# Stores of ScalarE's PSUM copies issued by ScalarE's own queue instead of SyncE's, in a hybrid RWKV-7, SSD and GLA block

## Chip, cores and metric

The kernel runs on one core of a Trainium2 chip. The metric is the device time of one execution in microseconds (us); three executions before the change had a median of 1492.69 us, from 1491.11 to 1495.21 us.

## What is computed

One trunk layer of a diffusion backbone, all in float32. A latent stream of 1024 tokens with 1024 channels and a context of 256 tokens are normalized, projected by one matrix, and handed to three groups of heads; the concatenated results go through an output projection and a residual, and a mixture of 16 experts (two per token) and a final norm follow. The change touches the RWKV-7 group, cut down here to what matters:

```python
def step(s, inp):                       # rwkv7_scan, 4 heads of 64, run forwards and backwards
    r_t, w_t, k_t, v_t, a_t, b_t = inp
    sa = jnp.einsum('bhvk,bhk->bhv', s, a_t)
    s = s * w_t[:, :, None, :] + sa[..., None] * b_t[:, :, None, :] + v_t[..., None] * k_t[:, :, None, :]
    return s, jnp.einsum('bhvk,bhk->bhv', s, r_t)
...
decay = exp(-exp(-softplus(-(w0[d] + wl @ w2[d])) - 0.5)); a = sigmoid(a0[d] + al @ a2[d])
kk = k * k_k / norm; scan_inputs = (r, decay, k * (1 + (a - 1) * k_a), v, -kk, kk * a)
```

## The kernel before

The scan is computed in chunks of 64 tokens. `rw_seg` prepares a segment of 256 tokens (four chunks) for one pair of heads (b, 0 or 1) and both directions (d). There are five segments, so `rw_seg` goes 20 times through its inner loop; each such pass is called a segment pass here. In a segment pass TensorE transposes v into `ptv`, ScalarE copies it out of PSUM into `vt` (L433), and SyncE stores it to DRAM as `vtD` (L434). TensorE then makes `psl` in two halves (L438), ScalarE takes tanh into `sa` (L440), VectorE scans it into `cum` (L446), GpSimd subtracts (`cex`, L447), ScalarE takes three or four exps (L449 to L454), VectorE and GpSimd multiply them into `AR` and `BK`, and TensorE multiplies these into `psg` (L475), which VectorE masks into `G` (L477). GpSimd scales `BK` (L485), TensorE transposes it into `ptb` (L490), and ScalarE copies it into `BT` (L491), which has one buffer. SyncE stores `BT` to `stepD` by four DMAs of 64 KB (L496, here called a quartet). `AR` and `G` are stored by SyncE too (L481 to L483).

DRAM hands these results to later stages. `rw_inverse` reads `mabD` into `Dm`, inverts blocks on VectorE (lines L546 and L547 in turn, then the copy `DT`, L550), stores and reloads them as `t1` and `t2`, and multiplies them on TensorE as `px` (L575) and `px2` (L580). It runs three times; "inverse 2" is the one for positions 0 to 3 of both b, and the last but one in time. The scan loop `rw_step` reads `stepD` (L592) and `vtD` (L600); it begins when all jobs are through.

Around these, other jobs fill the engines: input projections (`psi`, L274 to L276, copied by ScalarE into `po` or `u`), convolutions (`co`, L751 on VectorE, after L740 on ScalarE), conditioning products (`psa`, L201, and `psc`, L206), and projections for GLA and SSD (`pst`, L274 to L276 as well). A job list fixes the order in which the program is written:

```python
PLAN = "s0 z0 z1 s1 z3 q0 z2 z5 z4 q1 c1 i0 g0 i2 c0 a4 a5 c3 a6 a7 c2 a8 a9 c5 a10 a11 t0 i1 c4"
...
with _tile.TileContext(nc, schedule_with_timeline_sim=True) as tc:
```

(s is a segment job with ten segment passes, i an inverse, c a convolution, a a conditioning product, t the GLA and SSD projection.) The order on each engine is not the written one. A scheduler takes the written program and decides when each instruction goes into its engine's line, so that a change of one queue can move instructions on all engines. Each engine runs its line strictly in order.

Of the kernel before, what the change touches and what calls it, by code (L numbers as in the profile page):

```python
# [48 lines left out]
def sigma(eng, out, t):  # L49

    eng.tensor_scalar(out, t, 0.5, 0.5, op0=OP.mult, op1=OP.add)
# [276 lines left out]
HS = [slice(0, 64), slice(64, 128)]  # L328


def chunks(t):
    return t.rearrange("p (c t) -> p c t", t=64)


def flip(v, d):
    return v[:, ::-1, ::-1] if d else v
# [76 lines left out]
def rw_seg(g, b, s, r, k, v, wa, kk):  # L413

    nc = g.nc
    t0, n, pos = SEGS[s]
    T = lambda tag, bufs=2, w=256: g.tmp.tile([128, w], F, tag=tag, name=tag, bufs=bufs)
    ts = slice(t0, t0 + n)
    r, k, v, wa, kk = r[:, ts], k[:, ts], v[:, ts], wa[:, ts], kk[:, ts]
    nch = n // 64  # L420
    for d in range(2):
        p0, bd = pos[d], 2 * b + d
        pp = slice(p0, p0 + nch)
        if d:
            vd = T("sq")[:, 0:n]
            nc.scalar.activation(vd[:, ::-1], v, AF.Copy)
        else:
            vd = v
        pt = g.ps.tile([128, 4, 128], F, tag="tp", name="ptv")
        for i in range(n // 128):  # L430
            nc.tensor.transpose(pt[:, i, :], vd[:, 128 * i:128 * i + 128], g.ident)
        vt = T("vt", 2, 258)[:, 0:n].rearrange("p (i c) -> p i c", c=128)
        nc.scalar.activation(vt, pt[:, 0:n // 128], AF.Copy)  # L433
        nc.sync.dma_start(g.vtD[pp, :, 128 * bd:128 * bd + 128].rearrange("(i q) t c -> (q t) i c", q=2), vt)  # L434
        ps = g.ps.tile([128, 2, 256], F, tag="tp", name="psl")
        sa = T("sa", 2, 512).rearrange("p (q t) -> p q t", q=2)
        for q in range(2):
            nc.tensor.matmul(ps[:, q, :], g.wa2[64 * q:64 * q + 64, d, 128 * b:128 * b + 128],  # L438
                             wa[64 * q:64 * q + 64], start=True, stop=True)
            nc.scalar.activation(sa[:, q, :], ps[:, q, :], AF.Tanh, scale=0.5,  # L440
                                 bias=g.hb[:, 4 * q + 2 * d + b:4 * q + 2 * d + b + 1])
        sigma(nc.vector, sa, sa)
        sig, av = sa[:, 0, :], sa[:, 1, :]
        cum, cex = T("cum")[:, 0:n], T("cex")[:, 0:n]
        rv = (lambda x: x[:, ::-1]) if d else (lambda x: x)
        nc.vector.tensor_tensor_scan(rv(cum), g.m01[:, 0:n], rv(sig), 0.0, op0=OP.mult, op1=OP.add)  # L446
        nc.gpsimd.tensor_sub(cex, cum, sig)  # L447

        nc.scalar.activation(cex, cex, AF.Exp, scale=-KAPPA)  # L449
        dst = g.PC[:, bd, p0:p0 + nch]  # L450
        nc.scalar.activation(dst[:, ::-1] if d else dst, chunks(cum)[:, :, 0 if d else 63], AF.Exp, scale=-KAPPA)
        if s:
            nc.scalar.activation(sig, cum, AF.Exp, scale=-KAPPA)
        nc.scalar.activation(cum, cum, AF.Exp, scale=KAPPA)  # L454
        ar = T("AR", 2, 512).rearrange("p (c a t) -> p c a t", a=2, t=64)[:, 0:nch]
        nc.vector.scalar_tensor_tensor(flip(ar[:, :, 0, :], d), chunks(kk), -1.0, chunks(cex), op0=OP.mult, op1=OP.mult)
        if s:
            nc.gpsimd.tensor_mul(flip(ar[:, :, 1, :], d), chunks(r), chunks(sig))
        else:
            nc.gpsimd.tensor_copy(ar[:, :, 1, :], ar[:, :, 0, :])  # L460

        nc.vector.scalar_tensor_tensor(cex, av, 1.0, k, op0=OP.subtract, op1=OP.mult)
        nc.vector.scalar_tensor_tensor(cex, cex, g.c("ka", b), k, op0=OP.mult, op1=OP.add)
        nc.gpsimd.tensor_mul(av, av, kk)
        bk = T("BK", 2, 512).rearrange("p (c a t) -> p c a t", a=2, t=64)[:, 0:nch]
        for h in range(2):
            for q, x in ((h, av), (1 - h, cex)):
                nc.vector.tensor_mul(flip(bk[HS[h], :, q, :], d), chunks(x[HS[h]]), chunks(cum[HS[h]]))
        bkf, arf = bk.rearrange("p c a t -> p c (a t)"), ar.rearrange("p c a t -> p c (a t)")

        G = T("G", 2, 1024).rearrange("p (c h t) -> p c h t", h=2, t=128)[:, 0:nch]
        pg = [g.ps.tile([128, 4, 128], F, tag="gm", name="psg") for h in range(2)]
        for c in range(nch):
            for h in range(2):
                nc.tensor.matmul(pg[h][:, c, :], bkf[HS[h], c], arf[HS[h], c], start=True, stop=True)  # L475
        for h in range(2):
            nc.vector.tensor_mul(G[:, :, h, :], pg[h], g.mG[:, None, :].to_broadcast([128, 4, 128]))  # L477
        for h in range(2):
            o, u = HS[h], HS[1 - h]
            x0 = 384 * bd  # L480
            nc.sync.dma_start(g.mabD[b, o, pp, d], G[o, :, h, :])  # L481
            nc.sync.dma_start(g.stepD[o, pp, x0:x0 + 128], arf[o])
            nc.sync.dma_start(g.stepD[o, pp, x0 + 128:x0 + 256], G[u, :, h, :])  # L483

        nc.gpsimd.tensor_mul(bkf, bkf, g.PC[:, bd, p0:p0 + nch, None].to_broadcast([128, nch, 128]))  # L485
        bt = T("BT", 1, 512).rearrange("p (c t) -> p c t", t=128)[:, 0:nch]
        for c0 in range(0, nch, 4):
            pt = g.ps.tile([128, 4, 128], F, tag="gm", name="ptb")
            for c in range(4):
                nc.tensor.transpose(pt[:, c, :], bkf[:, c0 + c], g.ident)  # L490
            nc.scalar.activation(bt[:, c0:c0 + 4], pt, AF.Copy)  # L491
        for h in range(2):
            for q in range(2):

                x0 = 384 * bd + 256 + 64 * q
                nc.sync.dma_start(g.stepD[HS[h], pp, x0:x0 + 64], bt[HS[h ^ q], :, 64 * h:64 * h + 64])  # L496


def rw_bonus(g, b, r, k, v):
# [1267 lines left out]
def block_kernel(tc, a, out):  # L1767
# [37 lines left out]
    def seg_block(g, b):  # L1805
        k, r, v = rw_proj(g, 2 + b), rw_proj(g, b), rw_proj(g, 4 + b)
        kk = rw_norm(g, b, k)
        for s in range(5):
            rw_seg(g, b, s, r, k, v, wa, kk)
        rw_bonus(g, b, r, k, v)  # L1810
# [73 lines left out]
```

## Time and profile before

| what | value |
|---|---|
| median of 3 runs | 1492.69 us (1491.11 to 1495.21) |
| the profiled execution | 1493.58 us |
| its span | 1491.8 us |
| TensorE clock granted, mean | 0.914 of full speed |
| TensorE busy | 1325.7 us (89%) |
| VectorE busy | 742.0 us (50%) |
| ScalarE busy | 517.6 us (35%) |
| GpSimd busy | 381.3 us (26%) |

PE stands for TensorE, PEld for its weight loads, DVE for VectorE, ACT for ScalarE, POOL for GpSimd and SP for SyncE; SPq and ACTq are the queues in which those engines issue DMAs. Issuing a DMA is not counted as busy, though the engine can do nothing else in that time. The 1.8 us between the span and the execution's time lie outside the engines' program.

### The profile page before, as it was taken

What the parts mean: (1) busy time and instruction counts of PE and PEld (TensorE: products, weight loads), DVE (VectorE), ACT (ScalarE), POOL (GpSimd) and SP (SyncE); (2) the same over time, 40 slices, a digit from 0 to 9 for tenths busy, and PEclk for the clock granted to TensorE, in tenths of its full rate; (3) what the DMA queues carried; (4) which work ended last, traced back from release to release, by engine and by line L of the source; (5) the groups of instructions that cost most, each with busy time, mean ns of one, the idle gap of its engine ahead of it and who ended that gap; (6) DMA issues with size and microseconds to landing.
All of it is one profiled execution on the core that took longest, in us unless ns stands there. A gap on an engine that the chain in (4) does not pass through costs nothing. (4 is left out here: it accounts for less than half of the span.)

```text
span 1491.8 us, 28106 instructions
## 1 busy us (share of the span) xinstructions
PE 1325.7 (89%) x11173; PEld 1089.7 (73%) x11173; DVE 742.0 (50%) x1421; ACT 517.6 (35%) x1062; POOL 381.3 (26%) x432
## 2 busy tenths in 40 slices
PE   6999999999897996687899889974999999999984
PEld 2487777777675675476477667754999999999984
DVE  4747768789697733524764652236112112112542
ACT  4545435533454033533542532212112212112323
POOL 3212342333332110423552431113001102101102
PEclk9999999999898887799875689996999999999997
DMA  9523667654867778487544544426998778778974
GB/s 281 188 86 87 133 139 169 161 126 106 156 180 187 222 196 236 146 249 223 180 147 131 146 160 146 159 96 220 362 348 275 239 257 288 260 262 295 321 249 126
DMA packets 297509, 296.07 MB, mean 198 GB/s; under 512 B 114153, under 2 KB 217194, under 8 KB 297375
## 3 DMA queue, kind: packets, MB, share of 16 engines
q1 hardware_dynamic: 288351, 269.07, 59.6%
q0 software_dynamic: 7872, 20.97, 5.9%
q10 hardware_dynamic: 1152, 4.19, 0.7%
q8 instruction: 90, 1.47, 0.4%
q14 instruction: 44, 0.36, 0.1%
HBM read 221.21 MB, written 73.49 MB: 198 GB/s over the span
## 5 line engine op out<-in xcount | busy, mean ns | idle before, releaser
L1592 PE MATMUL p<-hT,w 128*128 128x144 f32 (+10 forms) x2048 | 262.1, 287 | 0.0
L1592 PEld LDWEIGHTS p<-hT,w 128*128 128x128 f32 x2048 | 256.5, 192 | 0.6
L275 PE MATMUL psi<-hlo,whi 128*128 128x512 f32 (+1 forms) x440 | 168.8, 384 | 3.2 <-DVE hlo L247 1.8
L274 PE MATMUL psi<-hhi,whi 128*128 128x512 f32 (+1 forms) x440 | 168.7, 385 | 0.7 <-ACT po L693 0.5
L276 PE MATMUL psi<-hhi,wlo 128*128 128x512 f32 (+1 forms) x440 | 167.5, 381 | 0.0
L1599 PE MATMUL p<-hid,w 128*128 128x144 f32 (+10 forms) x1024 | 133.0, 289 | 10.5 <-DVE hid L1594 8.1
L1599 PEld LDWEIGHTS p<-hid,w 128*128 128x128 f32 x1024 | 130.1, 193 | 11.2 <-DVE hid L1594 8.6
L1618 POOL DMA_INDIRECT acc<-yr,rows x27 | 41.4, 1533 | 322.2 <-DVE yr L1614 188.2
L275 PEld LDWEIGHTS psi<-hlo,whi 128*128 128x128 f32 x440 | 84.4, 192 | 25.1 <-issue 5.0
L1594 DVE TENSOR_TENSOR hid<-hid,p 128x144 f32<-128x144 f32 (+10 forms) x64 | 18.8, 294 | 168.5 <-PE p L1592 161.4
L274 PEld LDWEIGHTS psi<-hhi,whi 128*128 128x128 f32 x440 | 84.4, 192 | 21.3 <-issue 5.3
L276 PEld LDWEIGHTS psi<-hhi,wlo 128*128 128x128 f32 x440 | 84.4, 192 | 19.1 <-issue 4.5
L1614 DVE TENSOR_SCALAR yr<-pty,rows 128x512 f32<-128x512 f32 (+8 forms) x46 | 32.7, 741 | 112.4 <-PE pty L1608 112.4
L1600 ACT ACTIVATE yT<-p,mods 128x144 f32<-128x144 f32 (+10 forms) x128 | 42.5, 375 | 109.4 <-PE p L1599 108.9
L1593 ACT ACTIVATE hid<-p 128x144 f32<-128x144 f32 (+10 forms) x64 | 18.3, 285 | 166.9 <-PE p L1592 166.8
L751 DVE SCALAR_TENSOR_TENSOR co<-gr,pc,co 128x512 f32<-128x512 f32 x72 | 61.5, 872 | 13.2 <-ACT co L740 12.2
L275 PE MATMUL pso<-wol,mh 128*128 128x512 f32 x128 | 52.1, 407 | 3.1 <-DVE wol L1238 3.1
L274 PE MATMUL pso<-woh,mh 128*128 128x512 f32 x128 | 51.9, 408 | 2.6 <-DVE rb L1253 1.7
L276 PE MATMUL pso<-woh,ml 128*128 128x512 f32 x128 | 52.2, 408 | 0.0
L475 PE MATMUL psg<-AR,BK 64*128 64x128 f32 x320 | 45.8, 292 | 3.9 <-ACT BT L491 2.1
L1559 ACT ACTIVATE hT<-pte,mods,gs 128x128 f32<-128x128 f32 (+4 forms) x76 | 27.5, 448 | 61.9 <-PE pte L1555 61.9
L475 PEld LDWEIGHTS psg<-AR,BK 64*128 64x128 f32 x320 | 38.3, 194 | 14.1 <-issue 5.7
(543 smaller groups left out, 2611.9 us busy)
## 6 DMA issues: line engine op xcount, KB each, us to landing
w<-in_moe_w_dram SPq DMA_DIRECT2D x47, 2048.0 KB
wada<-in_ada_w_dram SPq DMA_DIRECT2D x32, 512.0 KB
cd<-stepD SPq DMA_DIRECT2D x20, 768.0 KB
wraw<-in_w_in_dram SPq DMA_DIRECT2D x24, 512.0 KB
aw<-in_ada_w_dram SPq DMA_DIRECT2D x10, 512.0 KB
stepD<-AR SPq DMA_DIRECT2D x40, 128.0 KB
mabD<-G SPq DMA_DIRECT2D x40, 128.0 KB
stepD<-G SPq DMA_DIRECT2D x40, 128.0 KB
```

The source lines that it names most:

```text
L274: nc.tensor.matmul(ps, whi(k), xhi(k), start=k == 0, stop=False)
L275: nc.tensor.matmul(ps, whi(k), xlo(k), start=False, stop=False)
L276: nc.tensor.matmul(ps, wlo(k), xhi(k), start=False, stop=k == 7)
L475: nc.tensor.matmul(pg[h][:, c, :], bkf[HS[h], c], arf[HS[h], c], start=True, stop=True)
L751: nc.vector.scalar_tensor_tensor(o, src(dy, dx), w(3 * dy + dx), o, op0=OP.mult, op1=OP.add)
L1559: nc.scalar.activation(hT[:, k, c0:c0 + m], pt[:, j, 0:m], AF.Identity, scale=g.gs2[:, k:k + 1], bias=g.mods[:, 24 + k, 0:1])
L1592: nc.tensor.matmul(p[:, 0:n], w[:, k, fs], hT[:, k, s0:s0 + n], start=k == 0, stop=k == 7)
L1594: nc.vector.tensor_mul(hid[:, f, 0:n], hid[:, f, 0:n], p3[:, 0:n])
L1599: nc.tensor.matmul(p[:, 0:n], w2[:, f, 128 * k:128 * k + 128], hid[:, f, 0:n], start=f == 0, stop=f == 3)
L1600: nc.scalar.activation(yT[:, k, 0:n], p[:, 0:n], AF.Copy, scale=g.mods[:, 40 + k, 0:1])
L1614: nc.vector.tensor_scalar(yr[0:m, h], pf, wt[0:m, b:b + 1], None, op0=OP.mult)
L1618: nc.gpsimd.indirect_dma_start(out=g.acc, out_offset=bass.IndirectOffsetOnAxis(ap=rows[0:m, 0, b:b + 1], axis=0), in_=yr[0:m, :], in_offse ...
```

## The change

Two lines change the engine that issues a store: L434 (20 DMAs of 128 KB) and L496 (80 DMAs of 64 KB, in quartets). The data, their places in DRAM and the waits on them are the same.

```diff
--- before.py
+++ after.py
@@ -431,7 +431,7 @@
             nc.tensor.transpose(pt[:, i, :], vd[:, 128 * i:128 * i + 128], g.ident)
         vt = T("vt", 2, 258)[:, 0:n].rearrange("p (i c) -> p i c", c=128)
         nc.scalar.activation(vt, pt[:, 0:n // 128], AF.Copy)
-        nc.sync.dma_start(g.vtD[pp, :, 128 * bd:128 * bd + 128].rearrange("(i q) t c -> (q t) i c", q=2), vt)
+        nc.scalar.dma_start(g.vtD[pp, :, 128 * bd:128 * bd + 128].rearrange("(i q) t c -> (q t) i c", q=2), vt)
         ps = g.ps.tile([128, 2, 256], F, tag="tp", name="psl")
         sa = T("sa", 2, 512).rearrange("p (q t) -> p q t", q=2)
         for q in range(2):
@@ -493,7 +493,7 @@
             for q in range(2):
 
                 x0 = 384 * bd + 256 + 64 * q
-                nc.sync.dma_start(g.stepD[HS[h], pp, x0:x0 + 64], bt[HS[h ^ q], :, 64 * h:64 * h + 64])
+                nc.scalar.dma_start(g.stepD[HS[h], pp, x0:x0 + 64], bt[HS[h ^ q], :, 64 * h:64 * h + 64])
 
 
 def rw_bonus(g, b, r, k, v):
```

The scheduler then gives other orders on all engines, from the first segment passes up to the end of the scan's following stages; from the mixture of experts on they are the same again. Three places follow, word for word; the numbers behind the names tell buffers apart.

On ScalarE, in the segment passes of b = 0, before:

```order
L449 ACTIVATE cex_1316<-cex_1316 128x256
L453 ACTIVATE sa_1309<-cum_1315 128x256
L454 ACTIVATE cum_1315<-cum_1315 128x256
L491 ACTIVATE BT_1161<-ptb_1162 128x512
L440 ACTIVATE sa_1372<-psl_1371,hb_342 128x256
L433 ACTIVATE vt_1433<-ptv_1430 128x256
L265 ACTIVATE whi_2761<-wraw_2760 128x1024
L300 ACTIVATE u_1911<-psi_1947 128x512
L440 ACTIVATE sa_1372<-psl_1371,hb_342 128x256
L451 ACTIVATE PC_513<-cum_1378 128x4
```

and with the change, at the same segment passes:

```order
L433 ACTIVATE vt_1368<-ptv_1365 128x256
L434 DMA vtD_517<-vt_1368 128x2x128
L440 ACTIVATE sa_1309<-psl_1308,hb_342 128x256
L491 ACTIVATE BT_1161<-ptb_1162 128x512
L496 DMA stepD_514<-BT_1161 64x4x64 x4
L449 ACTIVATE cex_1316<-cex_1316 128x256
L451 ACTIVATE PC_513<-cum_1315 128x4
L453 ACTIVATE sa_1309<-cum_1315 128x256
L440 ACTIVATE sa_1372<-psl_1371,hb_342 128x256
L433 ACTIVATE vt_1433<-ptv_1430 128x256
```

The stores now stand in ScalarE's line: the quartet stands behind the copy into `BT_1161`, ahead of the next segment pass's exps (`cex_1316`, `sa_1309`) and the tanh of the one after it (`sa_1372`), and the store of `vt` stands ahead of a tanh as well. In 14 of the 20 segment passes the instruction behind the quartet is a tanh or an exp of a later pass.

On VectorE, at the end of the segment passes of b = 1, with the first inverse (`Dm_3320`) beside it, before:

```order
L550 COPY DT_3387<-Dm_3320 64x1024
L477 TENSOR_TENSOR G_2573<-psg_2575,mG_508 128x4x128
L456 SCALAR_TENSOR_TENSOR AR_2690<-kk_2071,cex_2683 128x4x64
L508 TENSOR_TENSOR bv_2736<-pbo_2734,rv_1973 128x256
L504 SCALAR_TENSOR_TENSOR rk_2739<-rv_1973,pc_337,k2_793 128x256
L462 SCALAR_TENSOR_TENSOR cex_2683<-sa_2676,k2_793 128x256
L463 SCALAR_TENSOR_TENSOR cex_2683<-cex_2683,pc_337,k2_793 128x256
L468 TENSOR_TENSOR BK_2696<-cex_2683,cum_2682 64x4x64 x2
L267 TENSOR_TENSOR wlo_4206<-wraw_4204,whi_4205 128x1024
L468 TENSOR_TENSOR BK_2696<-sa_2676,cum_2682 64x4x64 x2
L477 TENSOR_TENSOR G_2636<-psg_2637,mG_508 128x4x128
```

and with the change:

```order
L267 TENSOR_TENSOR wlo_4206<-wraw_4204,whi_4205 128x1024
L456 SCALAR_TENSOR_TENSOR AR_2690<-kk_2071,cex_2683 128x4x64
L477 TENSOR_TENSOR G_2636<-psg_2637,mG_508 128x4x128
L546 TENSOR_TENSOR Dt_3325<-Dm_3320 128x210
L504 SCALAR_TENSOR_TENSOR rk_2746<-rv_1973,pc_337,k2_793 128x256
L508 TENSOR_TENSOR bv_2743<-pbo_2741,rv_1973 128x256
L477 TENSOR_TENSOR G_2636<-psg_2638,mG_508 128x4x128
L462 SCALAR_TENSOR_TENSOR cex_2683<-sa_2676,k2_793 128x256
L547 TENSOR_TENSOR Dm_3320<-Dm_3320,Dt_3325 128x21x10
```

`G_2636`, the masking of a segment pass's products, stood behind the inverse's last step and its copy `DT`; it now stands ahead of the inverse's steps of 210 elements and after, and those come later.

On TensorE, at inverse 2 (`px_3750`), before:

```order
L206 MATMUL psc_4004<-sel_113,arow_4002 128x1 x4
L201 MATMUL psa_4146<-wada_4147,sgz_110 32x512 x2
L201 MATMUL psa_4146<-wada_4151,sgz_110 32x512 x2
L201 MATMUL psa_4146<-wada_4155,sgz_110 32x512 x2
L575 MATMUL px_3750<-t1_3740,t2_3741 32x32 x17
L274 MATMUL pst_4609<-thi_4535,hhi_83 128x280
L275 MATMUL pst_4609<-tlo_4536,hhi_83 128x280
L276 MATMUL pst_4609<-thi_4535,hlo_84 128x280
L274 MATMUL pst_4609<-thi_4535,hhi_83 128x280
```

with the change, first behind the same `psc_4004`:

```order
L275 MATMUL pst_4581<-tlo_4536,hhi_83 128x280
L276 MATMUL pst_4581<-thi_4535,hlo_84 128x280
L206 MATMUL psc_4004<-sel_113,arow_4002 128x1 x4
L201 MATMUL psa_4146<-wada_4147,sgz_110 32x512 x2
L201 MATMUL psa_4146<-wada_4151,sgz_110 32x512 x2
L201 MATMUL psa_4146<-wada_4155,sgz_110 32x512 x2
L201 MATMUL psa_4146<-wada_4159,sgz_110 32x512 x2
L206 MATMUL psc_4165<-sel_113,arow_4163 128x1 x4
L201 MATMUL psa_4171<-wada_4172,sgz_110 32x512 x2
```

and then, further on, at `px_3750` itself:

```order
L276 MATMUL pst_4637<-thi_4535,hlo_84 128x280
L274 MATMUL pst_4637<-thi_4535,hhi_83 128x280
L275 MATMUL pst_4637<-tlo_4536,hhi_83 128x280
L575 MATMUL px_3750<-t1_3740,t2_3741 32x32
L276 MATMUL pst_4637<-thi_4535,hlo_84 128x280
L575 MATMUL px_3750<-t1_3740,t2_3741 32x32 x31
L580 MATMUL px2_3751<-t1_3740,t2_3741 32x32
```

Four more rows of `psa` (eight instructions), the four `psc_4165` and 47 `pst` now stand ahead of `px_3750`, where ten of those `pst` stood inside it and the others behind it. The program has 45 reloads of ScalarE's tables before and 51 with the change, the additional ones in the GLA and SSD stages behind the scan.

## Rows read from the trace of the kernel before

**Rows 1.** The page: busy time, share of span and instructions of each engine.

```profile
PE 1325.7 (89%) x11173; PEld 1089.7 (73%) x11173; DVE 742.0 (50%) x1421; ACT 517.6 (35%) x1062; POOL 381.3 (26%) x432
```

**Rows 2.** Windows (us): busy time (x instructions) of each engine, granted clock, DMA share, GB/s.

```profile
150.00:250.00 100.00, 99.46 (x523) 77.77 (x521) 72.07 (x117) 42.26 (x91) 37.62 (x42) 1.00 0.70 151
350.00:375.00 25.00, 20.85 (x100) 16.22 (x100) 24.67 (x48) 7.06 (x15) 9.56 (x8) 0.93 0.47 100
375.00:400.00 25.00, 19.92 (x86) 16.59 (x86) 14.74 (x21) 12.21 (x20) 10.39 (x16) 0.73 0.78 158
450.00:475.00 25.00, 14.64 (x143) 11.31 (x143) 19.08 (x38) 9.74 (x17) 8.67 (x10) 0.75 0.70 193
...
795.00:820.00 25.00, 23.84 (x276) 17.80 (x278) 13.50 (x28) 7.01 (x14) 5.14 (x6) 0.50 0.34 106
```

**Rows 3.** Waits of PE from 100 to 350 us: total us, times, longest.

```profile
PE psi L274 <- ACT po L693: 0.5, 1, 0.5
```

**Rows 4.** One line's instructions, L496 and L434 on SP: ns minimum/median/maximum, first and last start.

```profile
L496 SPq DMA_DIRECT2D stepD<-BT x80: 574/608/1157, 155.8 to 393.7; - x80
...
L434 SPq DMA_DIRECT2D vtD<-vt x20: 365/551/565, 123.4 to 342.4; - x20
```

**Rows 5.** Timeline of SP from 200 to 213 us: start, duration, instruction.

```profile
200.96 2.55 SPq L496 DMA_DIRECT2D stepD<-BT  x4
```

**Rows 6.** Line L1721, the stores that ScalarE issues before the change.

```profile
L1721 ACTq DMA_DIRECT2D out_dram<-fx x8: 338/338/384, 1398.1 to 1457.4; - x8
```

**Rows 7.** Waits of SP's queue from 122 to 392 us.

```profile
SPq L496 <- ACT BT L491: 13.4, 6, 2.9
SPq L434 <- ACT vt L433: 12.9, 5, 5.5
```

**Rows 8.** Waits of ACT from 122 to 392 us.

```profile
ACT PC L451 <- DVE cum L446: 45.4, 18, 7.4
ACT sa L440 <- PE psl L438: 29.4, 18, 4.9
```

**Rows 9.** Timeline of ACT, two copies and exps of the segments.

```profile
200.36 0.58 ACT L491 ACTIVATE BT<-ptb 128x512 f32<-128x512 f32 x1
...
202.04 0.47 ACT L440 ACTIVATE sa<-psl,hb 128x256 f32<-128x256 f32 x1
...
211.25 0.42 ACT L449 ACTIVATE cex<-cex 128x256 f32<-128x256 f32 x1 [1.19 <-POOL cex L447]
```

**Rows 10.** Waits of PE from 350 to 560 us.

```profile
PE px L575 <- DMA t<-mabD: 10.4, 2, 8.5
...
PE ptb L490 <- DVE G L477: 3.9, 1, 3.9
...
PE psg L475 <- ACT BT L491: 2.1, 1, 2.1
```

**Rows 11.** Timeline of PE around the first px of inverse 2.

```profile
456.38 0.29 PE L276 MATMUL pst<-thi,hlo 128*128 128x280 f32 x1
456.51 0.95 PE L206 MATMUL psc<-sel,arow 128*128 128x1 f32 x8
457.39 1.91 PE L201 MATMUL psa<-wada,sgz 128*32 128x512 f32 x12
467.77 0.31 PE L575 MATMUL px<-t,t 32*32 32x32 f32 x2 [8.48 <-DMA t<-mabD]
469.97 1.06 PE L575 MATMUL px<-t,t 32*32 32x32 f32 x32 [1.89 <-DMA t<-mabD]
```

**Rows 12.** Timeline of DVE around the copy DT of inverse 2.

```profile
459.47 1.01 DVE L550 COPY DT<-Dm 32x1024 f32<-32x1024 f32 x1
...
478.53 3.65 DVE L751 SCALAR_TENSOR_TENSOR co<-gr,pc,co 128x512 f32<-128x512 f32 x5 [7.17 <-ACT co L740]
```

**Rows 13.** Groups on ACT: one reload of its tables before L384's square root.

```profile
L384 ACT ACT_TABLE_LOAD x7 | 9.0, 1283 | 0.1
```

## Prediction

> **What bounds the kernel now.** I read the page first: TensorE is busy for 1325.7 us, VectorE for 742.0 and ScalarE for 517.6 [rows 1]. A TensorE at 89% says that time can be gained in two ways only: by filling its idle stretches, or by a higher granted clock. So I went on to the windows, stage by stage. In the segment passes, TensorE works 99.46 of 100 us between 150 and 250 us, at full clock, VectorE 72 and ScalarE 42 [rows 2]. The waits of TensorE say the same: between 100 and 350 us it waits 0.5 us in all [rows 3]. Whatever SyncE is late with in that stage is hidden behind other matmuls.
>
> The end of that stage looks different. From 350 to 375 us VectorE is busy for 24.67 of 25 us and TensorE for 20.85; from 375 to 400 TensorE has 19.92 and a clock of 0.73; from 450 to 475 it has 14.64 at 0.75 [rows 2]. The waits of TensorE from 350 to 560 us name what ends the gaps: `px` waits 10.4 us for the loads of `t`, `ptb` 3.9 us for VectorE's `G`, `psg` 2.1 us for the copy into `BT` [rows 10]. No gap there ends with a store of `vt` or `BT`.
>
> **What the change removes from SyncE.** The quartets are 80 issues of 0.608 us median, 49 us, and the stores of `vt` 20 of 0.551 us, some 10 us [rows 4]: 59 us of SyncE's line between 123 and 394 us. SyncE also stood still in front of them, 13.4 us for `BT` and 12.9 us for `vt` [rows 7]; everything behind them in its line (loads of weights, stores of `AR` and `G`) waited with them. While TensorE waits 0.5 us in 250, none of that reaches the end, so for 100 to 350 us I cost the relief of SyncE at nothing. The matmuls that hide it are the projections; without them the 59 us would be the upper bound.
>
> **What it adds to ScalarE.** The same 100 issues. ScalarE issues only the eight last stores before the change, 338 ns each [rows 6]; SyncE needs 2.55 us for a quartet [rows 5]. So a quartet costs ScalarE between 4 × 0.338 = 1.35 and 2.55 us, at worst 4 × 1.157 = 4.6 [rows 4]; I take 2.55, since the shape is the same and not that of the last stores. Over 20 passes that is 51 us, with `vt` some 60. ScalarE has room for that in sum: 42 busy us in 100 [rows 2], and a segment pass lasts 13.5 us (270 us over 20), so ScalarE goes from some 6 to some 9. But it runs in order, and behind a quartet stands a tanh or an exp in 14 of 20 passes. For those VectorE (`cum`, `AR`, `BK`) and then TensorE (`psg`) wait. ScalarE now waits for others first: 45.4 us for `cum`, 29.4 us for `psl`, in 18 passes each, 4.2 us in a pass [rows 8]. A quartet that falls into such a wait is free. The timeline shows such places: after a copy into `BT` at 200.36 us the next tanh starts at 202.04, and `cex` at 211.25 after 1.19 us of idling [rows 9]. The bounds are 0 (all 20 in waits) and 51 us (none). I take **+4 us**: 2.55 minus 4.2 is below zero on average, so only passes with little waiting pay; at three of the 14, half of the quartet each, that is 3 × 1.3.
>
> **What the new order does.** At inverse 2, TensorE ends its `psa` at 459.30, then waits 8.48 us and 1.89 us for `t` [rows 11]. With the change eight more `psa` instructions (each two of the trace's rows, 12 of which take 1.91 us, so 16 × 0.16 = 2.5 us), four `psc` (0.95 us, as the eight of the row's, which are four instructions) and 47 `pst` (0.13 us from one start to the next, so 6.1 us at full clock and 12 at half) stand ahead: at least 9.6 us of work, about the whole gap. The opposite effect lies on VectorE: the copy `DT`, which stands at 459.47 us [rows 12] and on which the loads of `t` hang, has by the order some 7 us more of VectorE's work ahead of it, part of which moved in from behind. VectorE has idle time before and after (14.74 busy from 375 to 400 us [rows 2]; 7.17 us before the `co` at 478.53 [rows 12]), so part of the 7 us is absorbed. Bounds are 0 (the loads come as much later as the cover grows) and 10.4; I take **−6 us**.
>
> At the tail of the segment passes, `G` of the last but one pass comes ahead of the inverse's last steps. TensorE's waits for `G` and `BT` there, 3.9 + 2.1 [rows 10] and some 3 us of smaller ones, hang on it. Bounds are 0 and 9; I take **−4 us**, half, because VectorE is full there and only the order changes.
>
> Six more reloads of ScalarE's tables at 1.283 us [rows 13] are 7.7 us. They lie behind the scan, from 720 to 845 us, where TensorE has 23.84 of 25 us at a clock of 0.50 [rows 2] and ScalarE 7.01; other matmuls cover most. Bounds 0 and 7.7; I take **+1 us**.
>
> The sum is +4 − 6 − 4 + 1 = −5 us. The profiled execution took 1493.58 us, 0.9 above the median of 1492.69, so it gives 1488.6 beside the profile and 1487.7 beside the median: **1488 us**. A measurement of this kernel can tell about 0.3%, 4.5 us, from no change; the forecast lies just outside of it.
>
> A rule of the Trainium skill speaks against this change (DMA: Bandwidth & Descriptors, section "Issuing engines are not separate DMA queues"): DMAs started by different engines run on the same 16 DMA engines, and a second issuing engine saves only the first one's time to issue. By that rule the most to be had is SyncE's 59 us, and nothing where SyncE isn't waited for. The trace agrees as far as it goes: 0.5 us of TensorE's waiting in 250.
>
> **Rivals.** *No change.* The front hides both engines' issue time, the cover at inverse 2 is eaten by the later `DT`, and half of the tail's gain goes with ScalarE's quartets: −2 − 4 + 4 + 1 = −1, 1492 us, within 4.5 of before. For it speaks that VectorE is at 24.67 of 25 us [rows 2] where the tail's gaps are; against it, that 9.6 us of work move into a gap of 10.4.
>
> *Slower: ScalarE becomes the late engine of the segment passes.* The place is the 14 passes in which a quartet stands directly ahead of a tanh or an exp. TensorE has no spare time there [rows 2, 3], so a pass that comes late by more than its slack is lost in full. If half of each quartet isn't covered, that is 14 × 1.3 = 18 us; with −5 − 4 of the other terms (the quartets' +4 taken out: −9) it gives 1502 us, and without any gain 1511. It decides from the point at which the quartets' uncovered part passes 0.65 us a pass (9 us over 14). For it speaks that the fences on ScalarE show quartet and tanh close together; against it, 4.2 us of waiting in a pass [rows 8].
>
> *Slower by a shared path of issue.* If an issue takes longer while both engines issue, the quartet goes towards the longest that SyncE shows, 1.157 us an issue [rows 4], 4.6 us a quartet, above the 4.2 us of waiting. 20 × 2 us more, at half of them uncovered, is 20 us on top of −5: 1508 us. Nothing in the trace shows two engines issuing at once, so it gets a small share. The Trainium skill (Perfetto Trace Analysis, section "DMA Instruction — HWDGE (DVE, Sync)") describes one block that generates descriptors, for which a sequencer waits on a lock; the page names VectorE and SyncE, and no run here shows whether ScalarE meets the same block.
>
> *The gain is larger.* If both gaps close (−10.4 − 9) and TensorE keeps its full clock from 375 to 400 and 450 to 475 us, 1475 us.
>
> **How the numbers follow.** The forecast has a chance of 0.32, the larger gain 0.09, no change 0.28, ScalarE late 0.22, the shared path 0.09. So faster is 0.41, same 0.28, slower 0.31. The range reaches from the larger gain to between the two slower cases: 1475 to 1507 us. It leaves out the slower case without any gain (1511) and the bound of 51. The likeliest case alone, with its terms at half their bounds, has 1481 to 1491.
>
> **What would show it.** Right: no wait above 2 us of `px` for `t` at inverse 2; fewer waits for `G` and `BT` between 350 and 400 us; TensorE still near 99 of 100 us between 150 and 250; issues on ScalarE of about 0.6 us. Wrong: waits of `psg` or `ptb` for VectorE or GpSimd between 150 and 350 us, issues on ScalarE above 1 us, or the same gap at `px`, only later.

## The result and the profile after

The changed kernel takes 1536.16 us (median of four runs, 1530.65 to 1538.93) against 1493.95 for the kernel before in the runs beside it. The ratio is 1.0266, with a 95% interval of 1.0235 to 1.0296: slower by 42 us, far outside of the range of the forecast.

The page of the profiled execution, which answers to [rows 1]:

```profile
span 1537.1 us, 28071 instructions
...
PE 1352.7 (88%) x11173; PEld 1101.5 (72%) x11173; DVE 738.2 (48%) x1421; ACT 523.3 (34%) x1068; POOL 383.1 (25%) x432
```

TensorE has the same 11173 instructions and 27 us more busy time; VectorE has 4 us less. ScalarE's six additional instructions are the reloads of its tables. Windows of the stretches of [rows 2], with the same columns:

```profile
150.00:250.00 100.00, 100.00 (x503) 75.74 (x501) 69.50 (x113) 37.63 (x85) 36.43 (x41) 1.00 0.65 146
350.00:375.00 25.00, 22.93 (x127) 17.64 (x126) 24.86 (x45) 5.75 (x13) 8.97 (x9) 1.00 0.49 101
375.00:400.00 25.00, 16.43 (x60) 12.51 (x61) 22.74 (x41) 11.23 (x19) 11.66 (x13) 0.51 0.65 144
450.00:475.00 25.00, 20.69 (x109) 13.82 (x109) 23.07 (x47) 8.93 (x15) 7.09 (x9) 0.86 0.46 141
```

Between 150 and 250 us TensorE is busy for all 100 us, as before. The trace names no wait of TensorE at all between 100 and 350 us, against 0.5 us [rows 3]. From 375 to 400 us it has 16.43 us at a clock of 0.51, worse than before; from 450 to 475 us it has 20.69 at 0.86, better. The issues themselves, now in ScalarE's queue, and the waits of ScalarE from 122 to 400 us, which answer to [rows 4] and [rows 8]:

```profile
L496 ACTq DMA_DIRECT2D stepD<-BT x80: 582/628/1193, 156.2 to 406.8; - x80
```

```profile
L434 ACTq DMA_DIRECT2D vtD<-vt x20: 364/377/738, 124.5 to 347.0; - x20
```

```profile
ACT sa L440 <- PE psl L438: 32.0, 17, 4.9
ACT PC L451 <- DVE cum L446: 28.0, 13, 8.2
...
ACT sa L440 <- DMA stepD<-BT: 9.1, 3, 3.6
...
ACT cex L449 <- DMA stepD<-BT: 4.7, 2, 2.7
...
ACT th L704 <- DMA stepD<-BT: 2.7, 1, 2.7
ACT PC L451 <- DMA vtD<-vt: 2.4, 1, 2.4
...
ACT cum L454 <- DMA stepD<-BT: 1.9, 1, 1.9
```

A store of `BT` costs ScalarE 0.628 us, SyncE had needed 0.608; one of `vt` costs 0.377 against 0.551. Only 18.4 us of ScalarE's idle time end with a store of `BT` ahead of a tanh or an exp, in seven places (`sa`, `cex`, `cum`, and `th`, the tanh of another job).

That the engine can do nothing else while it issues, as was said ahead of the prediction, is not quite so. Rows of ScalarE's timeline:

```profile
210.21 0.48 ACT L440 ACTIVATE sa<-psl,hb 128x256 f32<-128x256 f32 x1 [1.33 <-DVE BK L468]
210.21 2.61 ACTq L496 DMA_DIRECT2D stepD<-BT  x4
...
401.13 6.29 ACTq L496 DMA_DIRECT2D stepD<-BT  x4
```

A tanh that went in just before the quartet runs beside its first issue. The last quartet takes 6.29 us in all, though none of its four issues takes more than 0.76: the rest are gaps between them.

So the segments lose little, 6 us. The rest is found by comparing when the same instruction starts in both traces, stage by stage. The names that mark a stage are the first `pa` (scan's start, L608), the last `py` (scan's end), the last `pkv` (end of the GLA states, L873), the first `pto` (output projection, L1285) and the first `p` of the experts (L1592):

| mark | before, us | after, us | later by |
|---|---|---|---|
| last `psg` of the segments | 387.4 | 393.8 | 6 |
| scan's start | 552.9 | 566.1 | 13 |
| scan's end | 713.4 | 736.1 | 23 |
| last `pkv` | 754.7 | 801.2 | 46 |
| output projection's start | 896.5 | 934.6 | 38 |
| first product of the experts | 1034.0 | 1073.1 | 39 |

Windows that are cut at these marks, first of before, then of after:

```profile
553.00:714.00 161.00, 122.97 (x2709) 102.41 (x2711) 70.99 (x155) 61.71 (x144) 47.84 (x48) 0.85 0.72 207
714.00:755.00 41.00, 34.17 (x240) 16.58 (x239) 32.21 (x52) 22.30 (x39) 28.76 (x23) 0.81 0.61 194
755.00:897.00 142.00, 128.20 (x1165) 98.78 (x1166) 79.03 (x134) 55.58 (x88) 49.85 (x47) 0.70 0.47 145
```

```profile
566.00:736.00 170.00, 127.87 (x2659) 106.81 (x2657) 57.91 (x137) 59.05 (x136) 42.91 (x43) 0.82 0.68 197
736.00:803.00 67.00, 49.11 (x394) 26.10 (x390) 49.48 (x83) 34.23 (x62) 42.17 (x34) 0.72 0.51 157
803.00:935.00 132.00, 115.40 (x1076) 86.98 (x1072) 66.18 (x120) 54.90 (x82) 42.43 (x40) 0.68 0.44 137
```

From the start of the experts to the end the profile loses another 6 us, in a part whose order is unchanged; I have no cause for these.

The scan takes 170 instead of 161 us, though TensorE works through about 50 matmul records less in it. The stretch behind it, up to the last `pkv`, takes 67 instead of 41 us: there are 394 instead of 240 records left for it, and TensorE is busy for 73% of it at a clock of 0.72, where it was 83% at 0.81. The next stage gives ten back. Over all three, TensorE has 7 us more of busy time (292.4 after 285.3) and 18 us more of idle time (76.6 after 58.7). What was moved is visible in the order of TensorE's line, where 92 of the 152 `pkv` stood among the scan's matmuls before, and 64 stand there now. The traces agree: at two rows a matmul, 60 `pkv` are left behind the scan's end before and 88 now.

```profile
713.60:756.00 42.40, 3.30 (x120) 1.61 (x120) 4.15 (x15) 0.80 0.60 189
```

```profile
736.30:802.00 65.70, 4.97 (x176) 2.46 (x176) 6.04 (x22) 0.71 0.52 159
```

In the stretch behind the scan the trace also names TensorE's waits. They grow from 6.7 to 17.8 us, above all those of `ptk`, the transposes that feed `pkv`: they wait for GpSimd's `kend`, and for VectorE's update `gS` of the state. First before (714 to 755 us), then after (736 to 803 us):

```profile
PE ptk L863 <- POOL kend L848: 1.9, 1, 1.9
```

```profile
PE ptk L863 <- POOL kend L848: 5.5, 2, 3.2
PE ptk L863 <- DVE gS L875: 4.0, 1, 4.0
```

### The profile page after: what moved, and what is told of

Same layout as the page of the kernel before. It is cut to its first block, busy times and chain, and to the rows that moved or that the text cites. A ratio compares the mean times of both kernels' runs of the same rounds, so it can differ in the third digit from the quotient of the medians.

```text
span 1537.1 us, 28071 instructions
## 1 busy us (share of the span) xinstructions
PE 1352.7 (88%) x11173; PEld 1101.5 (72%) x11173; DVE 738.2 (48%) x1421; ACT 523.3 (34%) x1068; POOL 383.1 (25%) x432
## 5 line engine op out<-in xcount | busy, mean ns | idle before, releaser
L1592 PE MATMUL p<-hT,w 128*128 128x144 f32 (+10 forms) x2048 | 263.8, 288 | 0.0
L1592 PEld LDWEIGHTS p<-hT,w 128*128 128x128 f32 x2048 | 258.2, 192 | 0.6
L1599 PEld LDWEIGHTS p<-hid,w 128*128 128x128 f32 x1024 | 132.5, 197 | 10.8 <-DVE hid L1594 9.2
```

What stands on the lines that cost most here:

```text
L1592: nc.tensor.matmul(p[:, 0:n], w[:, k, fs], hT[:, k, s0:s0 + n], start=k == 0, stop=k == 7)
L1599: nc.tensor.matmul(p[:, 0:n], w2[:, f, 128 * k:128 * k + 128], hid[:, f, 0:n], start=f == 0, stop=f == 3)
```

## The experiments

Two theories stood against each other. Theory A: the scheduler's new order costs the time, not the issues. Theory B: the issues block ScalarE's line, as in the rival of the forecast. They are told apart by holding an order. A function is called at the end of the program's text and ties each instruction of an engine to the one that is to stand ahead of it. The ties set the order of issue alone and add no semaphore:

```python
def hold(tc):
...
    info = mybir.DependencyInfo(mybir.DependencyClass.NoSync, mybir.DependencyReason.DATA)
    for names in order.values():
        names = [f"I-{n}" for n in names if f"I-{n}" in ins]
        for a, b in zip(names, names[1:]):
            tc.add_manual_dep(ins[b], a, info, reason="hold")
```

All results in one place; `pkv` is the count among the scan's matmuls by the order, of 152. "Reloads" are those of ScalarE's tables that the trace shows, 43 before. Each kernel's ratio is to runs of the kernel before that were taken beside it.

| kernel | stores on | order | `pkv` | reloads | last `pkv`, us | median, us | ratio (95% interval) |
|---|---|---|---|---|---|---|---|
| changed | ScalarE, 100 | its own | 64 | 49 | 801.2 | 1536.16 | 1.0266 (1.0235 to 1.0296) |
| e1 | ScalarE, 100 | before, held | 92 | 43 | 758.2 | 1495.58 | 1.0043 (1.0014 to 1.0072) |
| e2 | SyncE | changed, held | 64 | 49 | 800.1 | 1535.15 | 1.0317 (1.0280 to 1.0354) |
| e3 | ScalarE, 100 | from the scan on: before, held | 92 | 43 | 764.6 | 1504.11 | 1.0118 (1.0081 to 1.0155) |
| e4 | ScalarE, 20 | its own | 56 | 49 | 806.1 | 1526.69 | 1.0256 (1.0221 to 1.0291) |
| e5 | ScalarE, 100 | changed, held; 6 `v` | 64 | 49 | 793.3 | 1523.64 | 1.0240 (1.0197 to 1.0284) |
| e6 | SyncE | before, held; 6 `v` | 92 | 43 | 748.7 | 1491.16 | 1.0014 (0.9993 to 1.0035) |
| e7 | ScalarE, 1 | its own | 92 | 43 | 749.2 | 1495.09 | 1.0040 (1.0009 to 1.0072) |
| e8 | ScalarE, 1 | its own | 56 | 49 | 811.7 | 1534.29 | 1.0309 (1.0281 to 1.0337) |
| e9 | ScalarE, 100 | TensorE's scan and states: before, held | 92 | 43 | 764.3 | 1506.88 | 1.0125 (1.0078 to 1.0173) |
| e10 | SyncE | TensorE's scan and states: changed, held | 64 | 49 | 787.2 | 1517.48 | 1.0188 (1.0151 to 1.0226) |
| e11 | ScalarE, 100 | ahead of the scan: before, held | 92 | 43 | 760.3 | 1499.07 | 1.0046 (1.0022 to 1.0071) |

The count of reloads goes with that of `pkv` in every kernel, so no run tells the two apart. Six reloads at 1.283 us [rows 13] are 7.7 us of ScalarE's time. Even if nothing covered them, that would be far less than the 22 to 31 us that the order from the scan on costs (e2 and e3 below); they can be a part of it.

### e1 and e2: the issues and the order, each by itself

e1 is the changed kernel with the order of before held on all engines; the 100 stores are free to stand anywhere in ScalarE's line. e2 is its mirror image.

```diff
         block_kernel(tc, args, out)
+        hold(tc)
```

e1: 

> Stores of vt and BT on ScalarE as in the change, but every engine's other instructions are held in the order of the kernel before. Theory A (the new order costs the time, the issue itself is nearly free): 1485 to 1503 us, within 0.6% of before. Theory B (the 2.5 us that a quartet blocks ScalarE's line cost the time): at least 1515 us, with waits of TensorE's psg or VectorE for ScalarE between 150 and 400 us.

e2: 

> Stores on SyncE as before, but every engine's other instructions are held in the order of the changed kernel. Theory A (order): 1525 to 1545 us, as slow as the change. Theory B (issue on ScalarE): within 0.6% of before, 1485 to 1503 us.

e1 took 1495.58 us and e2 1535.15: with the stores on ScalarE and the old order nearly nothing is lost, with the stores on SyncE and the new order everything is. Theory B fell. What is left for the issues is the ratio of e1, 1.0043, or 6 us. Its trace shows the stores in ScalarE's queue, and which of ScalarE's waits in front of compute end with them:

```profile
L496 ACTq DMA_DIRECT2D stepD<-BT x80: 582/628/1712, 155.4 to 398.7; - x80
```

```profile
ACT cx L747 <- DMA stepD<-BT: 6.2, 1, 6.2
ACT sa L440 <- DMA stepD<-BT: 5.7, 3, 2.6
...
ACT whi L265 <- DMA stepD<-BT: 3.2, 1, 3.2
...
ACT vt L433 <- DMA stepD<-BT: 2.7, 1, 2.7
```

With a last one of 1.4 us they are 19.2 us in seven places. TensorE waits for ScalarE only 2.0 us between 100 and 350 us there. The scan of e1 starts at 557.5 us, 4.6 later than before. From the output projection to the end its profile loses another 6, in a part where the order is that of before. The profiled execution is the slowest of e1's eight, 1503.40 us against a median of 1495.58, and e3 loses nothing there, so I don't put that down to the stores.

### e3, e9, e10: where in the order

e3 holds the order of before only for what is written from the scan on. e9 holds only TensorE, and only the lines of the scan and of the GLA and SSD states. e10 does the same with the kernel before and the order of the changed one. The edit is that of e1 with fewer names in `order`.

e3: 

> The changed kernel with only the instructions written from the scan's steps on (scan, GLA, SSD, output projection and all behind) held in their order of before; projections, segments and inverses keep the order of the change. Theory A in the form that the stages behind the scan's start lose 25 of the 40 us: 1508 to 1515 us. Theory B, or the loss all in the segments and inverses: 1530 us or more.

e9: 

> The changed kernel; only TensorE's instructions of the scan and of the GLA and SSD states (1434 of its 7129 matmuls) are held in their order of before, so that 92 instead of 64 of the 152 pkv stand among the scan's steps. If that mix is what costs the late 30 us: 1500 to 1515 us. Rival, the other engines' order or SyncE's: 1528 us or more.

e10: 

> The mirror image: the kernel before with stores on SyncE; only the same instructions of TensorE are held in the order that they have with the change (64 pkv among the scan's steps). If that mix costs: 1508 to 1525 us. Rival: 1486 to 1498 us.

e3 took 1504.11 us, somewhat less than expected. The order from the scan on costs 31 us by the medians of e2 and e3 (1535.15 less 1504.11), and 22 us by the ratios of the changed kernel and e3 (1.0266 and 1.0118). e9 took 1506.88 and e10 1517.48. So holding one engine's order in one part of the program moves most of that, in both directions: it gives back 21 us to the changed kernel by the ratios (1.0266 to 1.0125; 29 us by the medians, which were measured at different times), and takes 28 us (1.88% of 1492.48; 25 by the medians) from the kernel before. Only TensorE's order is held in e9 and e10. What the other engines do was free to follow, and did: ScalarE's reloads went to 43 in e9 and to 49 in e10. The first and the last start of `pkv` in the traces of before, of the changed kernel, of e9 and of e10:

```profile
L873 PE MATMUL pkv<-vg,ke x304: 216/240/312, 614.1 to 754.7; 64*32 64x64 f32 x152
```

```profile
L873 PE MATMUL pkv<-vg,ke x304: 216/240/313, 627.7 to 801.2; 64*32 64x64 f32 x152
```

```profile
L873 PE MATMUL pkv<-vg,ke x304: 216/240/313, 624.5 to 764.3; 64*32 64x64 f32 x152
```

```profile
L873 PE MATMUL pkv<-vg,ke x304: 216/240/313, 610.9 to 787.2; 64*32 64x64 f32 x152
```

In e9 the last one starts at 764.3 us, though the first is as late as in e3; in e10 it starts at 787.2, though the first is earlier than in the kernel before.

The same windows as above, cut at the marks of e9 and of e10; of each the stretch behind the scan, and the sum from the scan's start to the output projection's:

```profile
726.00:765.00 39.00, 34.58 (x256) 17.09 (x258) 29.12 (x52) 21.86 (x38) 28.08 (x22) 0.82 0.55 176
...
sum 341.00, PE 282.41 PEld 216.17 DVE 178.21 ACT 142.00 POOL 129.31; mean PE 94.14 PEld 72.06 DVE 59.40 ACT 47.33 POOL 43.10
```

```profile
718.00:788.00 70.00, 53.02 (x405) 28.45 (x400) 51.01 (x83) 35.68 (x65) 42.92 (x35) 0.68 0.48 156
...
sum 366.00, PE 290.14 PEld 219.89 DVE 180.36 ACT 147.04 POOL 129.82; mean PE 96.71 PEld 73.30 DVE 60.12 ACT 49.01 POOL 43.27
```

TensorE idles for 58.6 us in e9, as before (58.7), and for 75.9 in e10, as in the changed kernel (76.6). The idle time thus moves with the held order. Which single wait carries it does not repeat: behind the scan of e10 the longest in sum is `pin` for ScalarE with 5.8 us, and `ptk` waits 3.6. Both profiled executions are the fastest of their four.

### e4, e7, e8: how little it takes

e4 moves the 20 stores of `vt` alone. e7 and e8 move one of these.

```diff
-        nc.sync.dma_start(g.vtD[pp, :, 128 * bd:128 * bd + 128].rearrange("(i q) t c -> (q t) i c", q=2), vt)
+        (nc.scalar if (b, s, d) == (1, 4, 1) else nc.sync).dma_start(g.vtD[pp, :, 128 * bd:128 * bd + 128].rearrange("(i q) t c -> (q t) i c", q=2), vt)
```

That is e8; e7 has (1, 2, 1).

e4: 

> Only the 20 stores of vt move to ScalarE; the order is the scheduler's own, another one than either. Theory A (order): anything from 1480 to 1540 us, not in proportion to 20 issues of 0.38 us. Theory B: 7.5 us of issue at most, so 1493 to 1501 us.

e7: 

> Only one of the 100 stores goes to ScalarE, that of vt in the pass b = 1, s = 2, d = 1; the scheduler's order differs from before in 1114 lines on TensorE all the same. Theory A (order): away from before by more than 0.6%, 1500 to 1530 us. Theory B (the cost of the issue): 0.4 us, so 1489 to 1498 us.

e8: 

> Only one of the 100 stores goes to ScalarE, that of vt in the pass b = 1, s = 4, d = 1; the order differs from before in 1485 lines on TensorE. Theory A: away from before by more than 0.6% (1500 to 1535 us), by another amount than with the store of s = 2. Theory B: 0.4 us, so 1489 to 1498 us.

e8 is the clearest of all: one issue of 0.409 us on ScalarE and a time of 1534.29 us, 3.1% above before.

```profile
L434 SPq DMA_DIRECT2D vtD<-vt x19: 366/551/565, 122.8 to 318.5; - x19
...
L434 ACTq DMA_DIRECT2D vtD<-vt x1: 409/409/409, 336.7 to 336.7; - x1
```

```profile
L873 PE MATMUL pkv<-vg,ke x304: 216/240/313, 632.3 to 811.7; 64*32 64x64 f32 x152
```

e7 missed what theory A expected: its order differs in over a thousand of TensorE's lines too, but the kernel takes 1495.09 us, 1.0040 of before. A different order isn't enough; e7 keeps 92 `pkv` in the scan, e4 and e8 have 56.

### e5 and e6: a wait that I took for the cause

In the scan of the changed kernel SyncE waits 24.8 us at L600 for `py` to release a buffer of `v` (10.8 before), and TensorE's `pa` waits for `cd`, whose loads stand behind. Both kernels have their own order held and six buffers:

```diff
-    v = T.tile([128, 4, 64], F, tag="v", name="v", bufs=3)
+    v = T.tile([128, 4, 64], F, tag="v", name="v", bufs=6)
```

e5: 

> The changed kernel, held in its own order on every engine, with six buffers instead of three for the scan's tile v, so that SyncE doesn't wait at L600 for py to release one while the loads of cd stand behind it. If that wait (24 us on SyncE in the scan) makes the scan's loads late: 1520 to 1529 us, with the waits of pa and py for cd at 10 us or less. Rival, the scan is slow for another reason (the order on TensorE itself): 1531 to 1541 us.

e6: 

> The kernel before, held in its own order, stores on SyncE, with six buffers for v. The same wait is 11 us there, and pa and py wait 7.6 us for cd: 1484 to 1490 us if the wait at L600 is what makes these late; 1489 to 1497 us, no change, if it isn't. It also shows whether holding an order costs anything by itself.

The waits of TensorE and of SyncE in the scan, of the changed kernel and of e5:

```profile
PE pa L608 <- DMA cd<-stepD: 14.4, 8, 3.8
PE pa L608 <- issue: 7.3, 2, 4.6
```

```profile
SPq L600 <- PE py L608: 24.8, 9, 4.5
SPq L592 <- PE py L608: 5.1, 4, 3.1
```

```profile
PE pa L608 <- issue: 10.4, 3, 4.5
PE pa L608 <- DMA cd<-stepD: 9.2, 5, 3.1
```

```profile
SPq L592 <- PE py L608: 26.9, 10, 5.5
```

The wait moved one load on, from `v` to `cd` itself (L592, 26.9 us), which has two buffers; `pa` still waits 19.6 us for `cd` and for what the trace doesn't name ("issue"), in place of 21.7. e5's time of 1523.64 us lies in the range that was expected, but its ratio, 1.0197 to 1.0284, overlaps with that of the changed kernel. So the wait for `v` isn't shown to cost anything. e6 doesn't differ from before (0.9993 to 1.0035), so holding an order and six buffers together cost nothing that can be told from noise.

### e11: another order that isn't slow

e11 holds only what is written ahead of the scan, with all stores on ScalarE. Behind that the scheduler chose freely and put 92 `pkv` and 28 `pss` (the SSD states) among the scan's matmuls, against 92 and 20 before, and 64 and 28 in the changed kernel.

> The changed kernel (all 100 stores on ScalarE) with only the instructions written ahead of the scan held in their order of before; behind it the scheduler is free, and puts 92 pkv and 28 instead of 20 pss among the scan's steps. If the mix in the scan decides: 1485 to 1503 us, as with the whole order held. Rival, any order other than that of before loses some 2%: 1515 us or more.

It took 1499.07 us, as fast as e1 within the intervals. So 28 `pss` instead of 20 do no harm as long as 92 `pkv` stand there. No run moves the `pkv` alone, so they mark the slow orders here and are not shown to be the whole of the cause. No version was found that is faster than the kernel before.

## Why the prediction was wrong

**The step that failed** is the pricing of the new order from the scan on. It was one term, +1 us, for six reloads of ScalarE's tables "from 720 to 845 us", with the sentence that "other matmuls cover most", read from one window of 25 us. That part of the order costs 22 us (changed kernel and e3, by the ratios) to 31 us (e2 and e3, by the medians). Nothing was said of what stands among the scan's matmuls. Fewer `pkv` stand there, and the rest are done later: in the stretch of 67 us behind the scan TensorE idles for 18 us, 7 before, at a clock of 0.72. That TensorE's order in the scan and the states decides most of it is shown by e9 and e10, with the other engines following. That the `pkv` do it because less is left to run beside them is argued, and the share of the six reloads, which take 7.7 us themselves, is open.

All of the signs that the prediction named for being right came true: `px` waits 0.6 us at inverse 2, the waits for `G` and `BT` between 350 and 400 us fell from 7.8 to 1.3 us, TensorE is busy for 100 of 100 us, and an issue on ScalarE takes 0.628 us in the median, one of the 80 over 1 us. Every one of them lies ahead of the scan, so they could not see the loss.

**The quartets, +4 us**, were right in kind and nearly in size. e1 gives 6 us (interval 2 to 11), and that includes the stores of `vt` and what the relief of SyncE gave. The bound of 51 us was far off: ScalarE's waits take up most of the stores, as the prediction had it from [rows 8], and TensorE waits for ScalarE only 2.0 us between 100 and 350 us in e1.

**The rival of a late ScalarE** came nearest to the sign, and is refuted as a mechanism: e2 is as slow without any store on ScalarE. **The rival of a shared path of issue** fails as a price for all quartets: the median went from 0.608 to 0.628 us with both engines issuing, and 19 of the 20 quartets take 2.6 to 3.3 us in the changed kernel, not 4.6. One goes beyond it, the last with 6.29 us at 401.13. In e1, e3, e5, e9 and e11 too one of the last four takes 6.0 to 7.0 us, where SyncE's longest was 3.13. `gc` on ScalarE waits 5.8 us behind it; what holds it up is open.

**Inverse 2, −6 us**, failed. The wait of `px` for `t` did shrink, from 10.4 to 0.6 us at inverse 2. But `psa` waits 9.0 us for its loads instead of 4.2, and the copies `DT` come later than before: by 32 us at the first inverse, 23 at inverse 2 (482.63 after 459.47 [rows 12]) and 19 at the last.

```profile
PE psa L201 <- DMA wada<-in_ada_w_dram: 9.0, 5, 3.9
...
PE px L575 <- DMA t<-mabD: 2.9, 2, 2.3
```

```profile
494.27 1.19 PE L575 MATMUL px<-t,t 32*32 32x32 f32 x62 [0.59 <-DMA t<-mabD]
```

```profile
482.63 1.08 DVE L550 COPY DT<-Dm 32x1024 f32<-32x1024 f32 x1
```

```profile
L550 DVE COPY DT<-Dm x3: 1014/1033/1078, 372.2 to 519.5; 64x1024 f32<-64x1024 f32 x2, 32x1024 f32<-32x1024 f32 x1
```

```profile
L550 DVE COPY DT<-Dm x3: 1085/1097/1107, 404.0 to 538.5; 64x1024 f32<-64x1024 f32 x2, 32x1024 f32<-32x1024 f32 x1
```

I had looked at inverse 2 alone and at some 7 us of VectorE's work; the steps of the first inverse, behind which the others stand, went back by 32. The scan starts 13 us later than before, of which e1 explains 4.6. **The tail, −4 us**, failed with it: the masks `G` come earlier, as the order shows, and the waits for them shrink, but others take their place (`pbo` for `rk` 4.2 us, `ptb` and `psg` for `BK` 4.4), and TensorE has 16.43 us at a clock of 0.51 from 375 to 400 us. Together these two terms were −10; the early order costs 8.5 us by e3 less e1 (1504.11 − 1495.58).

The three parts, 6 (e1 over before), 8.5 (e3 over e1) and 31 (e2 over e3), must add up to the 46 us of e2 over before, since each step starts where the last one ends; that they do is no check. The check is that the changed kernel, with its stores on ScalarE, lies 42 us above before in its own runs, close to e2, whose stores are on SyncE.

The rule of the Trainium skill that was weighed (DMA: Bandwidth & Descriptors, section "Issuing engines are not separate DMA queues") held: relieving SyncE of 59 us of issue gained nothing that any run shows.

## What to carry to other kernels

Where a scheduler orders the program, a change of one queue is two changes, and they have to be measured apart: hold the old order with the new queue, and the new order with the old queue. An order can be read before it is run, and the count that went with the time here, how many independent matmuls stand among the steps of a long recurrence, was in it; the places where the first differences are seen were not the ones that cost most. A loss of some per cent after a small edit says nothing about the edit until its order is held.

## What the runs showed that I had not expected

One store of 0.409 us on another engine moves the time by 3.1% (e8), while a hundred of them move it by 0.4% when the order is held (e1). A store of `vt` is cheaper on ScalarE's queue than on SyncE's, at a median of 0.377 against 0.551 us, while a store of `BT` isn't (0.628 against 0.608). And one quartet of twenty takes over 6 us on ScalarE's queue in the changed kernel, e1, e3, e5, e9 and e11.
